# Four edits to the token-mixing stage of a two-layer decoder trunk: order of the chunk products, query sums in four column groups, a centred v, small projections in halves

## The chip, the cores and the metric

The kernel runs on one core of a Trainium2 chip. The metric is the device time in microseconds of one execution; lower is better. The core has TensorE (matmuls; "PE", with its weight loads as "PEld"), VectorE ("DVE"), ScalarE ("ACT"), GpSimd ("POOL") and SyncE ("SP"), which issues most of the transfers. Matmuls write to PSUM; VectorE and ScalarE move results from there to SBUF.

## The reference

Two layers, each a half-step SwiGLU block, a token-mixing block, and another half-step SwiGLU block, all on 512 tokens of width 1024 in float32. Only the mixing block is touched. It projects the normed tokens once and runs three kinds of heads side by side: sliding-window attention, RWKV-7 time mixing and a short gated convolution. What the change touches:

```python
q = rms_norm(q.reshape(B, T, ATT_Q_HEADS, HEAD_DIM), q_gain)      # 8 heads of 64
...
w_log = -softplus(-(w0 + tanh(wd) @ w_w2)) - 0.5                  # small projections of width 64
a = sigmoid(a0 + ad @ a_w2)
...
def step(S, inp):                                                 # state S: v x k, per head
    s_kk = einsum('bhvk,bhk->bhv', S, kk_t)
    S = (S * w_t[:, :, None, :] - s_kk[..., None] * (kk_t * a_t)[:, :, None, :]
         + v_t[..., None] * k_t[:, :, None, :])
    return S, einsum('bhvk,bhk->bhv', S, r_t)
...
mean = jnp.mean(y, axis=-1, keepdims=True)                        # over the 64 of a head
var = jnp.mean(jnp.square(y - mean), axis=-1, keepdims=True)
y = ((y - mean) * rsqrt(var + RWKV_GN_EPS)).reshape(...) * gn_w + gn_b
bonus = jnp.sum(r * k * r_k, axis=-1, keepdims=True) * v
y = (y + bonus) * g
```

Each row of the state S belongs to one element of v, and all rows go through the same linear step. So if the mean over a head's v is taken off every v_t before the recurrence, the mean of y over the head is zero at every step.

## The kernel before

Tokens lie along the free dimension (512 columns), channels along the 128 partitions. The mixing stage of a layer (`mix`) is a set of Python generators that a loop at its end advances in turn: `products` (the large input and output projections, the filler), `rwkv(0)` and `rwkv(1)` (two pairs of 64-wide time-mixing heads, one chain each) and `attention`. Each `yield` of a chain names a cost in microseconds; the loop lets `products` take as many steps as that cost buys, by `RWKV_WORK`, `ATT_WORK` and `FILL_WORK`. That sets the order in which instructions are traced; a scheduler in the build then fixes the order on every engine, letting earlier-traced instructions that it deems ready go first. Each engine runs its own list in order. A block under `tc.manual_schedule` keeps the order of TensorE's instructions within the block; `behind(m, other)` adds a dependence so that a group of matmuls becomes ready at once.

Products (`projector`, helper `mm6`, L98, and in other parts `mm3`, L90 to L92) split each operand into a high and a low part and take three matmuls of 128 x 128 weights and 256 moving columns for each half of the tokens. All small matmuls of the mixing stage are plain fp32; the trace shows two matmul instructions for each of them. Transposes show one.

What the change touches, in order of the work:

- In `products`, after the tiles of k and v come four query tiles, two heads each. A tile's square is summed over each head's 64 channels: four matmuls (one for each block of 128 tokens) with the squares as weights and the two-column constant `bones2` as the moving side (L615), then a square root on ScalarE (L616). `rq`, with tokens on partitions, is used in the softmax.
- `rwkv(q)` begins with two small projections, `ps_w` (L682) on partitions 0 to 63 and `ps_a` (L684) on 64 to 127.
- `pairs` (L733 to L747) multiplies, for each of 8 chunks of 64 tokens and each of the 2 heads, a 64 x 64 weight with 128 moving columns. `e` is the head and so the half of the array's rows; `c` is the chunk's parity and so the half of its columns. It runs twice a chain (`B`, `K`).
- `vN` (L799) is v with tokens on partitions: four transposes (`tmajor`, L784) and a ScalarE copy (`tcopy`, L789). `ps_xv` (L805) and the state products `ps_gn` and `ps_o` read it. The eliminations (L770, L771), 15 pairs of small VectorE instructions, invert 16 x 16 blocks in the meantime.
- `ps_s` (L889) and `ps_ys` (L895) carry the state over the chunks and give `y`. Then the head mean is summed with the constant `bones` (`headsum`, L539, tile `ps_m`) and taken off (L900); the variance follows in the same way (`ps_v`), then scale, shift, bonus and gate, ending at L916. The last output products need the `y` of both chains.

Of the kernel before, what the change touches and what calls it, by code (L numbers as in the profile page):

```python
# [11 lines left out]
AF = mybir.ActivationFunctionType  # L12
ALU = mybir.AluOpType
AXL = mybir.AxisListType
ORDER = mybir.DependencyInfo(mybir.DependencyClass.Sync, mybir.DependencyReason.DATA)

P = 128
D = 1024
T = 512
# [6 lines left out]
NB = T // P  # L26
CH = 64
NC = T // CH
HB = math.exp(-0.5) / 2
BASE = 16  # L30
PAD = 24
GAP = 448
GROUPS = ((0, 12), (12, 22))
RWKV_WORK, ATT_WORK, FILL_WORK = 29.8, 15.2, 129.6
# [2 lines left out]
def _columns(spec):  # L37
# [11 lines left out]
    ("cw", 6),  # L49
))  # L50
CON, NCON = _columns((
    ("ident", P), ("bones", P), ("bones2", 2), ("su", CH), ("iu", CH), ("diag", CH),
    ("lev0", CH), ("lev1", CH), ("i64", CH), ("mc", P), ("mp", P), ("mq", P),
))

# [2 lines left out]
def trunk_kernel(ctx, tc, ins, out, layers=L, phases=("ffn1", "mix", "ffn2")):  # L58
    nc = tc.nc
# [11 lines left out]
    tt, stt, ts = nc.vector.tensor_tensor, nc.vector.scalar_tensor_tensor, nc.vector.tensor_scalar  # L71
    act, mm = nc.scalar.activation, nc.tensor.matmul
# [7 lines left out]
    def psum(shape, name, tag="x"):  # L80
        return ps.tile(shape, F32, name=name, tag=tag, bufs=2)
# [27 lines left out]
    HALVES = (slice(0, T // 2), slice(T // 2, T))  # L109
    rows = (slice(0, CH), slice(CH, P))  # L110
# [4 lines left out]
    con = const.tile([P, NCON], F32, name="con")  # L115
# [18 lines left out]
    vals = {}  # L134
# [9 lines left out]
    def cst(name):  # L144
        a, b = CON[name]
        return con[:, a:b]
# [366 lines left out]
    def mix(l, hn, ss, mp, then):  # L513
# [17 lines left out]
        def EA(name):  # L531
            return mp.tile([P, T], F32, name=name, tag="ea", bufs=3)
# [4 lines left out]
        def headsum(src, name, tag="x"):  # L537
            pt = psum([P, T], name, tag)
            mm(pt, cst("bones"), src, start=True, stop=True)  # L539
            return pt  # L540
# [7 lines left out]
        blocks = lambda t: t.rearrange("p (b c) -> p b c", c=P)  # L548

        lw = mp.tile([P, 2 * P], F32, name="lw", tag="lw")  # L550
# [6 lines left out]
        k_, r_, v_, yr = {}, {}, {}, {}  # L557
# [8 lines left out]
        def products():  # L566
# [12 lines left out]
            pt = yield from tile_()  # L579
# [6 lines left out]
            sq = EA("ksq")  # L586
# [8 lines left out]
            pt = yield from tile_()  # L595
# [7 lines left out]
            nc.scalar.copy(V, pv)  # L603
            qr = mp.tile([P, 4, T], F32, name="qr", tag="qr")
            rq = small("rq", NB * 8)
            rq4 = rq.rearrange("p (b i g) -> p b i g", i=4, g=2)
            for i in range(4):
                pt = yield from tile_()
                nc.scalar.copy(qr[:, i], pt)
                sq = EA("qsq")  # L610
                act(sq, pt, AF.Square)
                yield
                pq = psum([P, NB, 2], "ps_q")
                for b in range(NB):
                    mm(pq[:, b], sq[:, b * P : (b + 1) * P], cst("bones2"), start=True, stop=True)  # L615
                act(rq4[:, :, i], pq, AF.Sqrt, bias=vals["eps64"])  # L616
            nc.vector.reciprocal(rq, rq)
            got.update(kt=kt, V=V, qr=qr, rq=rq)
            done.add("att")
# [14 lines left out]
            for q in range(2):  # L634
                pt = yield from tile_()
                cc = EA("conv_c")
                nc.scalar.copy(cc, pt)
                pt = yield from tile_()
                u = EA("conv_u")
# [5 lines left out]
                pt = yield from tile_()  # L645
# [12 lines left out]
            for i in range(KD - 2):  # L658
                w = load_w(wo1[l, i, :, :6], 6)
                pt = psmm()  # L660
# [13 lines left out]
        def rwkv(q):  # L674

            R = f"r{q}"
            c1 = slice(q, q + 1)
            cw = slice(q * P, (q + 1) * P)
            lo = got["lo"]

            pw = psum([P, T], "ps_w", R)
            mm(pw, lw[:64, cw], lo[:64], start=True, stop=True)  # L682
            pa = psum([P, T], "ps_a", R)
            mm(pa, lw[64:, cw], lo[64:], start=True, stop=True)  # L684
            yield 1.7
            kp = prm(l, "kk")[:, c1]
            sq = EQ(q, "kksq")
# [45 lines left out]
            def pairs(src, name, other):  # L733
                M = U(q, name, [P, 2, NB, 2, CH])
                pts = [psum([P, NB, 2, CH], "ps_c", R) for _ in range(2)]
                with tc.manual_schedule(engines={mybir.EngineType.PE}):
                    for b in range(NB):
                        for c in range(2):
                            n = 2 * b + c
                            for e in range(2):  # L740
                                m = mm(pts[e][rows[c], b], src[rows[e], n * CH : (n + 1) * CH], AR[rows[e], :, n], start=True, stop=True)
                                behind(m, other)
                msk = con[:, CON["su"][0] : CON["iu"][1]].unsqueeze(1).to_broadcast([P, NB, 2 * CH])
                for e in range(2):
                    other = tt(M[:, e].rearrange("p b a t -> p b (a t)"), pts[e].rearrange("p b a t -> p b (a t)"), msk, ALU.mult)
                yield 1.4
                return M, other  # L747
# [10 lines left out]
            for c in range(2):  # L758
                for m in range(NM):
                    n = (c * NM + m) * 2 * NB  # L760
# [6 lines left out]
            for s in range(BASE - 1):  # L767
                n = BASE - 1 - s
# [18 lines left out]
            def tcopy(src, name):  # L787
                t = blocks(S(q, name))
                nc.scalar.copy(t, tmajor(src, "ps_" + name))  # L789
                return t  # L790
# [5 lines left out]


            K_, other = yield from pairs(ka, "K", other)
            vN = tcopy(v_[q], "vN")  # L799
            yield 0.4  # L800
            px = psum([P, 2, NB, CH], "ps_xv", R)
            for e in range(2):
# [93 lines left out]
            tt(chunks(y)[:, 1:], chunks(y)[:, 1:], pt[:, 1:], ALU.add)  # L896
            yield 1.2

            pm = headsum(y, "ps_m", R)
            stt(y, pm, -1.0 / CH, y, ALU.mult, ALU.add)  # L900
            yield 0.9
            sq = EQ(q, "gnsq")
            act(sq, y, AF.Square)
            pv = headsum(sq, "ps_v", R)
# [310 lines left out]
def lay_out(i):  # L1215
    import numpy as np

    a = {}
    c = np.ascontiguousarray
    a["xT"] = c(i["x"][0].T).reshape(KD, P, T)  # L1220
    a["cT"] = c(i["c"].reshape(KD, P).T)


    wT = i["w_ada"].reshape(L, D, 9, KD, P).transpose(0, 2, 3, 4, 1)
    a["wadaT"] = c(wT)
    last = i["w_ada"][0, :, :D].reshape(KD, P, 4, 2, P)[:, :, :, 1].transpose(2, 1, 0, 3).reshape(4, P, D)
    a["wa0"] = c(np.stack([wT[0, 1, ::2], wT[0, 1, 1::2], wT[0, 0, ::2], last], axis=2))
    a["crep"] = c(np.broadcast_to(i["c"].reshape(1, D), (P, D)))
    for n, w in (("w1", "w_ffn1_in"), ("w2", "w_ffn2_in")):
        a[n + "i"] = c(i[w].reshape(L, KD, P, 2, NF, P)[:, :, :, :, :8].transpose(0, 4, 3, 2, 1, 5))  # L1230
        wp = i[w].reshape(L, 2, 4, P, 2, NF // 2, 2, P).transpose(0, 5, 4, 1, 3, 6, 2, 7)
        a[n + "p"] = c(wp.reshape(L, NF // 2, 2, 2, P, KD, P))
    for n, w in (("w1o", "w_ffn1_out"), ("w2o", "w_ffn2_out")):
        a[n] = c(i[w].reshape(L, NF, P, KD, P).transpose(0, 3, 2, 1, 4))

    pairs = np.concatenate([np.r_[g * CH : (g + 1) * CH] for t in range(4) for g in (t, 4 + t)])
    rw = lambda j: np.r_[768 + j * P : 768 + (j + 1) * P]
    cv = lambda j: np.r_[1792 + j * P : 1792 + (j + 1) * P]  # L1240
    order = [np.r_[512:768], pairs] + [rw(j) for j in (6, 2, 0, 4, 3, 1, 5, 7)]
    order += [cv(j) for j in (2, 4, 0, 3, 5, 1)]
    wm = i["w_mix_in"][:, :, np.concatenate(order)]
    a["wmi"] = c(wm.reshape(L, KD, P, 20, P).transpose(0, 3, 2, 1, 4))
    wo = i["w_mix_out"]
    w1 = wo[:, np.concatenate([pairs, np.r_[768:1024], np.r_[512:768]])]
    a["wmo1"] = c(w1.reshape(L, KD, P, KD, P).transpose(0, 3, 2, 1, 4))
    w2 = wo[:, 512:768, : 6 * P].reshape(L, 2, P, 2, 3, P)
    a["wmo2"] = c(w2.transpose(0, 3, 2, 4, 1, 5).reshape(L, 2, P, 6, P))
    a["lora"] = c(np.concatenate([i["rwkv_w_w2"], i["rwkv_a_w2"]], axis=1))  # L1250
    a["gw2"] = c(i["rwkv_g_w2"])

    def cols(v, n):
        return v.reshape(L, n, P).transpose(2, 0, 1)

    def twice(v):
        return np.concatenate([v, v], axis=1).T[:, :, None]

    sinks = i["att_sinks"][:, [0, 4, 1, 5, 2, 6, 3, 7]]
    a["par"] = c(np.concatenate([  # L1260
        cols(i["b_ada"], 72), cols(i["g_ffn1"], 8), cols(i["g_mix"], 8), cols(i["g_ffn2"], 8),
        twice(i["att_q_gain"]), twice(i["att_k_gain"]), np.broadcast_to(sinks[None], (P, L, 8)),
        cols(i["rwkv_mu"], 8), cols(i["rwkv_w0"], 2), cols(i["rwkv_a0"], 2), cols(i["rwkv_k_k"], 2),
        cols(i["rwkv_k_a"], 2), cols(i["rwkv_r_k"].reshape(L, 256), 2), cols(i["rwkv_gn_w"], 2),
        cols(i["rwkv_gn_b"], 2), cols(i["conv_w"].reshape(L, 768), 6),
    ], axis=2))


    r, s = np.arange(P)[:, None], np.arange(P)[None, :]
    u, v = r % CH, np.arange(CH)[None, :]  # L1270

    def lower(k, u, v):
        return (u >> (k + 1) == v >> (k + 1)) & ((u >> k) & 1 == 1) & ((v >> k) & 1 == 0)

    con = [r == s, r // CH == s // CH, r // CH == np.arange(2)[None, :], u < v, u <= v]
    con += [u // BASE == v // BASE, lower(4, u, v), lower(5, u, v)]
    con += [u == v, r <= s, r > s, s <= r]
    a["con"] = c(np.concatenate([np.asarray(x, np.float32) for x in con], axis=1))
    return a
# [16 lines left out]
```

## Time and profile before

| | |
|---|---|
| median of 3 runs | 1936.84 us (1936.34 to 1939.99) |
| profiled execution | 1942.73 us, span 1940.6 us |
| granted TensorE clock, mean | 0.990 |
| TensorE busy | 1894.4 us, 98% of the span |
| VectorE busy | 1400.0 us, 72% |
| ScalarE busy | 838.4 us, 43% |
| HBM traffic | 302.66 MB read, 3.41 MB written |

The time of an execution is a little longer than the span, which runs from the first to the last instruction. A busy TensorE includes matmuls that wait in its pipeline, so 98% does not say that the array works at its peak. The mixing stages lie at about 400 to 625 us and 1350 to 1576 us of the span. A line such as `ps_q<-con,qsq` names the tile written and the tiles read.

### The profile page before, as it was taken

How to read it: one execution, taken by the hardware profiler on the slowest of the kernel's cores; microseconds unless marked ns; L12 is line 12 of the kernel's file. 1: busy time of each engine (PE TensorE's matmuls, PEld its weight loads, DVE VectorE, ACT ScalarE, POOL GpSimd, SP SyncE). 2: the span in 40 equal slices, each digit the busy share in tenths (PEclk: the TensorE clock that was granted, in tenths of full speed). 3: DMA queues.
4: the chain of work that ended last, by engine and by line, in shares of the span. 5: the costliest groups of instructions: out<-in, count | busy, mean ns of one | idle time of the engine just before them, and what ended most of it. 6: DMA issues, size and time to landing. Idle time of an engine off the chain costs nothing. (4 is left out here: it accounts for less than half of the span.)

```text
span 1940.6 us, 36814 instructions
## 1 busy us (share of the span) xinstructions
PE 1894.4 (98%) x15392; PEld 1748.4 (90%) x15392; DVE 1400.0 (72%) x2176; ACT 838.4 (43%) x1269; POOL 130.8 (7%) x212
## 2 busy tenths in 40 slices
PE   8999999999999999999999999999999999999999
PEld 7998899797889999899899989988978899998997
DVE  7687687658975787677877776876588578773762
ACT  4443255347422554155345514544562235532551
POOL 0101101000000000110100020010000000010100
PEclk8999999999999999999999999999999999999999
DMA  7767875621222475886746688773222125765742
GB/s 296 250 161 232 258 197 170 211 69 47 54 60 63 133 203 168 279 216 173 227 123 180 171 263 234 184 221 97 88 54 57 51 61 153 205 218 131 197 113 90
DMA packets 104325, 308.44 MB, mean 159 GB/s; under 512 B 23392, under 2 KB 24416, under 8 KB 103136
## 3 DMA queue, kind: packets, MB, share of 16 engines
q1 hardware_dynamic: 75936, 203.34, 32.5%
q0 software_dynamic: 28224, 102.77, 21.5%
q8 instruction: 120, 1.97, 0.4%
q14 instruction: 45, 0.37, 0.1%
HBM read 302.66 MB, written 3.41 MB: 158 GB/s over the span
## 5 line engine op out<-in xcount | busy, mean ns | idle before, releaser
L101 ACT CAST wH<-wraw 128x1024 fp32r<-128x1024 f32 (+2 forms) x292 | 268.9, 922 | 561.7 <-PE ps_mm L91 157.5
L102 DVE TENSOR_TENSOR wL<-wraw,wH 128x1024 fp32r<-128x1024 f32 (+2 forms) x292 | 309.0, 1060 | 123.3 <-ACT wH L101 121.8
L91 PE MATMUL ps_mm<-actL,wH 128*128 128x512 f32 (+1 forms) x744 | 282.5, 380 | 0.0
L90 PE MATMUL ps_mm<-actH,wH 128*128 128x512 f32 (+1 forms) x744 | 282.5, 380 | 0.0
L92 PE MATMUL ps_mm<-actH,wL 128*128 128x512 f32 (+1 forms) x744 | 282.0, 379 | 0.0
L380 PE MATMUL ps_d<-comH,wH 128*128 128x256 f32 x816 | 227.6, 279 | 4.5 <-ACT s L402 3.8
L381 PE MATMUL ps_d<-comL,wH 128*128 128x256 f32 x816 | 226.2, 277 | 0.0
L382 PE MATMUL ps_d<-comH,wL 128*128 128x256 f32 x816 | 226.1, 277 | 0.0
L98 PE MATMUL ps_mm<-hnH,wH 128*128 128x256 f32 x1040 | 213.8, 287 | 5.3 <-ACT hnH L101 2.9
L98 PE MATMUL ps_mm<-hnH,wL 128*128 128x256 f32 x1040 | 213.9, 285 | 0.5 <-DVE wL L102 0.5
L98 PE MATMUL ps_mm<-hnL,wH 128*128 128x256 f32 x1040 | 212.5, 284 | 0.0
L163 DVE SCALAR_TENSOR_TENSOR wada<-wada,crep 128x1024 f32<-128x1024 f32 x140 | 167.8, 1221 | 53.8 <-DMA wada<-in_wadaT 53.6
L102 DVE TENSOR_TENSOR wL<-sum,wH 128x1024 fp32r<-128x1024 f32 x102 | 125.0, 1225 | 70.1 <-ACT wH L101 69.9
L98 PEld LDWEIGHTS ps_mm<-hnH,wH 128*128 128x128 f32 x1040 | 160.8, 191 | 13.6 <-issue 5.5
L101 ACT CAST wH<-sum 128x1024 fp32r<-128x1024 f32 x102 | 107.5, 1054 | 148.0 <-PE ps_d L381 72.1
L98 PEld LDWEIGHTS ps_mm<-hnH,wL 128*128 128x128 f32 x1040 | 161.2, 191 | 6.3 <-issue 4.7
L98 PEld LDWEIGHTS ps_mm<-hnL,wH 128*128 128x128 f32 x1040 | 161.6, 191 | 4.5 <-issue 3.9
L92 PEld LDWEIGHTS ps_mm<-actH,wL 128*128 128x128 f32 x744 | 141.2, 190 | 26.1
L91 PEld LDWEIGHTS ps_mm<-actL,wH 128*128 128x128 f32 x744 | 141.2, 190 | 25.6
L90 PEld LDWEIGHTS ps_mm<-actH,wH 128*128 128x128 f32 x744 | 140.9, 189 | 25.7
L380 PEld LDWEIGHTS ps_d<-comH,wH 128*128 128x128 f32 x816 | 153.9, 189 | 7.1 <-ACT s L402 5.0
L381 PEld LDWEIGHTS ps_d<-comL,wH 128*128 128x128 f32 x816 | 154.1, 189 | 0.0
(401 smaller groups left out, 4245.5 us busy)
## 6 DMA issues: line engine op xcount, KB each, us to landing
wada<-in_wadaT POOLq DMA_DIRECT2D x128, 512.0 KB, 5.0
wraw<-in_wmi SPq DMA_DIRECT2D x40, 512.0 KB
wraw<-in_w2p SPq DMA_DIRECT2D x36, 512.0 KB
wraw<-in_w1p SPq DMA_DIRECT2D x32, 512.0 KB
wraw<-in_w1o SPq DMA_DIRECT2D x32, 384.0 KB
wraw<-in_w2o SPq DMA_DIRECT2D x32, 384.0 KB
wraw<-in_w1i SPq DMA_DIRECT2D x20, 512.0 KB
wraw<-in_w1o SPq DMA_DIRECT2D x32, 320.0 KB
```

What stands on the lines that cost most here:

```text
L90: mm(acc, wH, xH, start=start, stop=False)
L91: mm(acc, wH, xL, start=False, stop=False)
L92: mm(acc, wL, xH, start=False, stop=stop)
L98: mm(acc[:, sl], w[a][:, k], x[b][:, sl], start=start and n == 0 and sl is HALVES[0], stop=stop and n == 2, skip_group_check=True)
L101: nc.scalar.copy(hi, src)
L102: nc.vector.tensor_sub(lo, src, hi.bitcast(F32))
L163: stt(w, w, 1.0, crep, ALU.mult, ALU.mult, accum_out=out_)
L380: mm(pt[:, i], wH, x[k][0], start=start and i + k == 0, stop=False, skip_group_check=True)
L381: mm(pt[:, i], wH, x[k][1], start=False, stop=False, skip_group_check=True)
L382: mm(pt[:, i], wL, x[k][0], start=False, stop=k == 3, skip_group_check=True)
```

## The change

Four edits, all in the mixing stage of both layers and both chains:

1. `pairs` loops over the head before the chunk's parity, so that neighbouring matmuls alternate between the column halves first.
2. The squares of all four query tiles are kept. One burst of four matmuls sums them, each with 32 columns of `bones` as weights (16 for each of the two heads) and 512 moving columns, each to its own 32 partitions. ScalarE copies the sums out, four transposes turn them, and one square root reads one of every 16 columns. `bones2` goes; `PAD` makes up for its two columns.
3. `vN` is centred when it is taken from PSUM: VectorE sums each head's 64 elements and subtracts the mean. The step that summed and subtracted the mean of `y` goes, with its `yield`. The bonus still reads the uncentred v.
4. The two small projections are cut in two halves of 256 tokens and issued alternately, in a fixed order.

```diff
@@ products
             rq = small("rq", NB * 8)
-            rq4 = rq.rearrange("p (b i g) -> p b i g", i=4, g=2)
+            sqs = []
             for i in range(4):
                 pt = yield from tile_()
                 nc.scalar.copy(qr[:, i], pt)
-                sq = EA("qsq")
-                act(sq, pt, AF.Square)
-                yield
-                pq = psum([P, NB, 2], "ps_q")
-                for b in range(NB):
-                    mm(pq[:, b], sq[:, b * P : (b + 1) * P], cst("bones2"), start=True, stop=True)
-                act(rq4[:, :, i], pq, AF.Sqrt, bias=vals["eps64"])
+                sqs.append(S(i % 2, "qsq"))
+                act(sqs[i], pt, AF.Square)
+            yield
+            pq = psum([P, T], "ps_q")
+            with tc.manual_schedule(engines={mybir.EngineType.PE}):
+                for i in range(4):
+                    mm(pq[32 * i : 32 * i + 32], cst("bones")[:, CH - 16 : CH + 16], sqs[i], start=True, stop=True)
+            qs = EA("qsum")
+            nc.scalar.copy(qs, pq)
+            yield
+            pq = psum([P, NB, P], "ps_qt")
+            for b in range(NB):
+                nc.tensor.transpose(pq[:, b], qs[:, b * P : (b + 1) * P], cst("ident"))
+            act(rq.rearrange("p (b i g) -> p b i g", i=4, g=2), pq.rearrange("p b (i g r) -> p b i g r", i=4, g=2)[:, :, :, :, 0], AF.Sqrt, bias=vals["eps64"])
             nc.vector.reciprocal(rq, rq)
@@ rwkv
-            pw = psum([P, T], "ps_w", R)
-            mm(pw, lw[:64, cw], lo[:64], start=True, stop=True)
-            pa = psum([P, T], "ps_a", R)
-            mm(pa, lw[64:, cw], lo[64:], start=True, stop=True)
+            pw, pa = (psum([P, T], n, R) for n in ("ps_w", "ps_a"))
+            with tc.manual_schedule(engines={mybir.EngineType.PE}):
+                for sl in HALVES:
+                    for pt, r in ((pw, rows[0]), (pa, rows[1])):
+                        mm(pt[:, sl], lw[r, cw], lo[r, sl], start=True, stop=True, skip_group_check=True)
@@ rwkv, pairs
                     for b in range(NB):
-                        for c in range(2):
-                            n = 2 * b + c
-                            for e in range(2):
+                        for e in range(2):
+                            for c in range(2):
+                                n = 2 * b + c
                                 m = mm(pts[e][rows[c], b], src[rows[e], n * CH : (n + 1) * CH], AR[rows[e], :, n], start=True, stop=True)
@@ rwkv
-            vN = tcopy(v_[q], "vN")
+            pt = tmajor(v_[q], "ps_vN").rearrange("p b (e d) -> p (b e) d", e=2)
+            mv = small(f"mv{q}", 2 * NB)
+            nc.vector.tensor_reduce(mv, pt, AXL.X, ALU.add)
+            vN = S(q, "vN")
+            stt(vN.rearrange("p (b d) -> p b d", d=CH), mv.unsqueeze(2).to_broadcast([P, 2 * NB, CH]), -1.0 / CH, pt, ALU.mult, ALU.add)
+            vN = blocks(vN)
@@ rwkv
-            pm = headsum(y, "ps_m", R)
-            stt(y, pm, -1.0 / CH, y, ALU.mult, ALU.add)
-            yield 0.9
             sq = EQ(q, "gnsq")
```

The constant table loses its `bones2` columns, and `PAD` goes from 24 to 26.

More of the change, by code (lines that the diff above doesn't have):

```diff
@@ L30 @@
 BASE = 16
-PAD = 24
+PAD = 26
 GAP = 448
@@ L51 @@
 CON, NCON = _columns((
-    ("ident", P), ("bones", P), ("bones2", 2), ("su", CH), ("iu", CH), ("diag", CH),
+    ("ident", P), ("bones", P), ("su", CH), ("iu", CH), ("diag", CH),
     ("lev0", CH), ("lev1", CH), ("i64", CH), ("mc", P), ("mp", P), ("mq", P),
@@ L1273, in lower @@
         return (u >> (k + 1) == v >> (k + 1)) & ((u >> k) & 1 == 1) & ((v >> k) & 1 == 0)
-    con = [r == s, r // CH == s // CH, r // CH == np.arange(2)[None, :], u < v, u <= v]
+    con = [r == s, r // CH == s // CH, u < v, u <= v]
     con += [u // BASE == v // BASE, lower(4, u, v), lower(5, u, v)]
```

## The prediction

> **What bounds the kernel now.** I read the page first, then the waits of TensorE, then stretches of the mixing stage, and last the timeline of TensorE around every burst that the change touches.
>
> ```profile
> PE 1894.4 (98%) x15392; PEld 1748.4 (90%) x15392; DVE 1400.0 (72%) x2176; ACT 838.4 (43%) x1269; POOL 130.8 (7%) x212
> ```
> ```profile
> PE ps_s L889 <- ACT y L884: 2.9, 2, 1.8
> ...
> PE ps_mm L98 <- DVE y L916: 0.5, 2, 0.3
> ```
> ```profile
> 480.00:520.00 40.00, 38.48 (x349) 31.11 (x348) 35.54 (x97) 21.71 (x54) 0.00 (x0) 1.00 0.21 52
> ```
> ```profile
> 1501.30:1511.50 10.20, 10.20 (x75) 8.29 (x75) 3.56 (x17) 1.27 (x3) 0.00 (x0) 0.50 0.04 9
> ```
> ```profile
> 550.20:560.00 9.80, 9.80 (x101) 8.10 (x98) 5.45 (x21) 3.45 (x8) 0.00 (x0) 1.00 0.07 12
> ```
>
> TensorE is busy 98% of the span, so a change is worth what it takes off TensorE's own sequence, minus any new gap. The waits (total, times, longest) show two small gaps that matter in mixing: ps_s waits for the eviction of y, 2.9 us in the two layers, and the last products wait 0.3 us a layer for the finished y of the second head pair. The third fence is a stretch of the first layer's mixing: the columns are length, then busy time of PE, weight loads, DVE, ACT, POOL, granted clock, DMA share, GB/s. DVE is busy 35.54 of 40 us there, close behind TensorE. The last two fences have the stretches right behind those gaps for ps_s: in the second layer, behind 1.8 us, the granted clock was 0.50 for 10.2 us, which costs 5.1 us of full-speed work; in the first, behind 1.1 us (2.9 less 1.8), it stayed at 1.00.
>
> The profiled execution took 1942.73 us, the median of the runs shown is 1936.84. Without that half-clock stretch it would be 1942.73 - 5.1 = 1937.6, next to the median, so I take it that the median run does not have the stretch, and set the sum against 1936.84. A measurement here can tell about 0.2%, 3.9 us, from no change.
>
> **How a burst is priced.** The products run as a stream of L98 matmuls, and small bursts break into it. The price of a burst is the time from a product row before it to one after it, less the products that started in that time. Two L98 matmuls take 0.23 us (612.19 to 612.42 below). So the price includes what it costs to enter and leave.
>
> **Query sums.** Before, each of four query tiles has a burst of its own: four fp32 sums, eight matmuls whose moving side is two columns wide. Columns: start, us, engine, line, what, count.
>
> ```profile
> 410.31 1.04 PE L615 MATMUL ps_q<-con,qsq 128*128 128x2 f32 x8
> 411.21 0.49 PE L98 MATMUL ps_mm<-hnH,wH 128*128 128x256 f32 x2
> ```
> ```profile
> 416.34 0.39 PE L98 MATMUL ps_mm<-hnL,wH 128*128 128x256 f32 x2
> 416.77 1.05 PE L615 MATMUL ps_q<-con,qsq 128*128 128x2 f32 x8
> 417.69 0.48 PE L98 MATMUL ps_mm<-hnH,wL 128*128 128x256 f32 x2
> 418.00 0.39 PE L98 MATMUL ps_mm<-hnH,wH 128*128 128x256 f32 x2
> ```
>
> The second burst costs 418.00 - 416.34 = 1.66, less four products (0.46), so 1.20 us. The first stands behind the transposes of v and shares their way in and out: 0.90 us from 410.31 to 411.21, of which I keep 0.80, since the transposes then have to leave by themselves. A layer has 0.80 + 3 x 1.20 = 4.40 us.
>
> After, one burst holds four matmuls of 128 rows x 32 columns with 512 moving columns, each in its own quarter of the columns, two passes each; then ScalarE copies the sums and four transposes turn them. No row has quarter-width column groups. The nearest is the attention's ps_av, two half-width groups with 512 moving columns; for the transposes it is ps_vN.
>
> ```profile
> 446.24 0.40 PE L98 MATMUL ps_mm<-hnL,wH 128*128 128x256 f32 x2
> 446.57 1.08 PE L990 MATMUL ps_av<-pmc,V 128*64 128x512 f32 x4
> 447.57 0.50 PE L98 MATMUL ps_mm<-hnH,wL 128*128 128x256 f32 x2
> 447.91 0.40 PE L98 MATMUL ps_mm<-hnH,wH 128*128 128x256 f32 x2
> ```
> ```profile
> 495.88 0.28 PE L98 MATMUL ps_mm<-hnH,wL 128*128 128x256 f32 x1
> 496.16 0.66 PE L784 MATMUL ps_vN<-con,v 128*128 128x128 f32 x4
> 496.57 0.37 PE L98 MATMUL ps_mm<-hnH,wL 128*128 128x256 f32 x1
> 496.77 0.40 PE L98 MATMUL ps_mm<-hnH,wH 128*128 128x256 f32 x2
> ```
> ```profile
> 612.19 0.39 PE L98 MATMUL ps_mm<-y2L,wH 128*128 128x256 f32 x2
> 612.42 0.40 PE L98 MATMUL ps_mm<-y2H,wL 128*128 128x256 f32 x2
> 612.65 1.02 PE L539 MATMUL ps_m<-y,con 128*128 128x512 f32 x2
> 613.11 0.80 PE L98 MATMUL ps_mm<-y3H,wH 128*128 128x256 f32 x2
> 613.75 0.39 PE L98 MATMUL ps_mm<-y3L,wH 128*128 128x256 f32 x2
> ```
>
> ps_av, four matmuls, costs 447.91 - 446.24 = 1.67 less 0.46, so 1.21 us. A single sum of the same width, ps_m, costs 613.75 - 612.42 = 1.33 less 0.46, so 0.87 us. Two of them apart would be 1.74; the two column groups ran together. I take 1.21 for the four quarters as well, because that row is the nearest; the other end is four in a row, 4 x 0.87 = 3.48. The transposes cost 496.77 - 495.88 = 0.89 less 0.23, so 0.66. New price of a layer 1.21 + 0.66 = 1.87, gain 4.40 - 1.87 = 2.53, **5.1 us for two layers**; at the other end 4.40 - 4.14 = 0.26 a layer, 0.5 us in all. The ScalarE copy between sums and transposes has the products as cover (one step is handed over there); two fewer steps are handed over in all, which only shifts the pacing. Scores need no rq, only the softmax does, so a later rq delays nothing at first.
>
> **No mean of y.** ps_m goes in two layers and two head pairs: 4 x 0.87 = **3.5 us off TensorE**. The DVE subtraction behind it goes too. In its place the eviction of ps_vN changes: one ScalarE copy becomes a DVE sum over the transposed v and a DVE subtraction.
>
> ```profile
> L900 DVE SCALAR_TENSOR_TENSOR y<-ps_m,y x4: 691/692/693, 557.6 to 1568.6; 128x512 f32<-128x512 f32 x4
> ...
> L953 DVE TENSOR_REDUCE mx<-Sc x16: 675/676/679, 435.2 to 1447.6; 128x4 f32<-128x512 f32 x16
> ...
> L789 ACT COPY vN<-ps_vN x4: 586/588/590, 496.9 to 1492.6; 128x512 f32<-128x512 f32 x4
> ```
>
> By these forms the step takes 0.676 + 0.692 instead of 0.588: 0.78 us longer before ps_xv can start, and 1.37 us more of DVE at that place, 0.69 less at the end. Behind it on DVE wait the softmax steps and the 16-row eliminations of the same head pair. Free it would be 0; exposed four times 4 x 0.78 = 3.1 us. The first pair's falls into the stretch where DVE is 89% busy, the second's behind it; so I charge 0.78 once a layer, **1.6 us**.
>
> **Small projections by halves.** Before, they ran apart for the first pair and together for the second:
>
> ```profile
> 461.18 1.12 PE L682 MATMUL ps_w<-lo,lw 64*128 64x512 f32 x2
> 462.23 0.66 PE L972 MATMUL ps_pt<-con,Sc 128*128 128x128 f32 x4
> 462.82 1.12 PE L684 MATMUL ps_a<-lo,lw 64*128 64x512 f32 x2
> ```
> ```profile
> 481.38 0.69 PE L682 MATMUL ps_w<-lo,lw 64*128 64x512 f32 x1
> 481.38 0.69 PE L684 MATMUL ps_a<-lo,lw 64*128 64x512 f32 x1
> ...
> 482.44 0.34 PE L741 MATMUL ps_c<-AR,a 64*64 64x128 f32 x4
> ```
>
> Transposes of the attention were put between ps_w and ps_a: 1.05 us each (461.18 to 462.23). The pair together takes 482.44 - 481.38 = 1.06. With the order held and the row halves alternating, the first pair saves 1.05 us a layer, **2.1 us**. If something is still put between after the first half, one quarter runs alone at each end: half of it, 1.05. The second pair gains nothing.
>
> **Chunk products, columns first.** The same matmuls in another order:
>
> ```profile
> 484.27 0.88 PE L741 MATMUL ps_c<-AR,a 64*64 64x128 f32 x22
> ```
> ```profile
> 542.31 0.30 PE L861 MATMUL ps_gn<-vN,kaN 64*64 64x64 f32 x8
> ```
>
> In the old order four of them last 0.34 us (the row at 482.44 above) and 22 are through in 0.88 us, so four run at a time: 18 more in 0.54 us is 0.12 us for every four. The ps_gn loop already has the new order (same rows, other columns next); with half the moving columns its eight are through in 0.30 us. Both orders fill the array; I take 0. If the new order ran two abreast, the eight fours of a call would take 0.12 us more each, 1.0 us a call and 7.7 us for the eight calls: the bad end. A tenth of that the other way, 0.8 us, is my good end, an estimate without a row.
>
> **The sum.** -5.1 - 3.5 - 2.1 + 0 + 1.6 = -9.1: 1936.84 - 9.1 = **1927.7 us**. Against the profiled execution's own time, half-clock stretch included, that is 1933.6.
>
> **Rivals.** *Column groups wait for each other.* Then the query sums give 0.5 instead of 5.1: 1927.7 + 4.6 = 1932.3 us. Against it stands ps_av. The Trainium skill, TensorE: Matmul & The Clock Gate, Part 3, states that a weight load overlaps a running matmul only where its row group differs, and quarters of the columns share all rows. By that rule this rival would be the forecast; ps_av and ps_gn, whose neighbours share rows and start together, speak against it for halves, and no row shows quarters.
>
> *A gap and the half clock (the other side).* ps_s waits because DVE works on the other pair's eliminations ahead of the eviction. If the added 1.37 us of DVE lengthens that gap in both layers and the clock falls each time as at 1501.30, this costs 2 x (1.4 + 5.1) = 13: 1927.7 + 13 = 1940.7, and with any further gap slower than 1936.84 + 3.9. It decides only if both layers do it in most runs; in one layer it gives 1934.2. For it: it happened once in the profile. Against: the shorter gap of the first layer left the clock at 1.00, and between the transposes of v (496.16) and that gap (ahead of 550.20) lies some 50 us of other work that can take up a delay. The Trainium skill, TensorE: Matmul & The Clock Gate, Part 1, has the clock fall only after an idle window of about 3.4 us; the trace has it fall behind a gap of 1.8 us, so I let the trace decide. By the page the rival would lose its 5.1 us a layer and end at 1930.5.
>
> *The chain becomes the end.* TensorE is freed of 10.7/2 = 5.3 us a layer, the second pair's chain only of 0.87 + 0.69 - 0.78 = 0.78, if its head does not move forward with the rest. Then products wait for y 4.5 us a layer: the row with 0.3 us grows, and -9.1 - 1.6 + 9.0 = -1.7 gives 1935.1 (the 1.6 charged above is in the 9.0). For it: that wait exists in both layers, so chain and products end together. Against: query sums and small projections lie ahead of the chain and move its head too.
>
> *Better.* The new order of work closes the ps_s gap: 2.9 us more, and 0.8 from the pairs, and part of the half-clock stretch where runs have it: about 1922.
>
> **Chances.** Forecast 0.49, columns wait 0.10, gap in one layer 0.13, in both 0.08, chain 0.12, better 0.08. Faster by over 0.2% (below 1933.0) are the forecast, the first rival, the better case and the upper part of the others, 0.69; within 0.2% are the chain and the single gap, 0.23; slower 0.08. The range 1922 to 1936 takes in the bounds and leaves out the double gap and half of the better case. The forecast's own range is 1924 to 1932.
>
> **What the profile after would show.** One ps_q burst a layer, four 32-column matmuls of two passes started within some 0.02 us of each other and a price near 1.2 us; started half a microsecond apart, the first rival. No ps_m, and y squared right after its last addition. ps_w and ps_a of the first pair together, about 1.06 us in all. The ps_c bursts as long as before. If ps_s or the product row behind L916 waits longer, or the half-clock share grows, the second or third rival holds. What would make the forecast wrong without any of them is a wholly new order of TensorE's work, in which other bursts are cut apart.

## The result and the profile after

Over 20 runs of each kernel the median went from 1936.81 us (1929.83 to 1942.88) to 1928.76 us (1920.99 to 1936.80): ratio 0.9964, 95% interval 0.9951 to 0.9976. In a later comparison it was 0.9942 (0.9922 to 0.9963). The forecast was 1927.7 us, so size and sign were right. Term by term it was not: the query sums gave less than forecast, the small projections about nothing on their own, the longer step of v showed no cost, and a gap that the sum had left in place closed.

The head of the page of the kernel after, profiled in an execution of 1928.72 us, and its waits (total, times, longest):

```profile
span 1926.7 us, 36742 instructions
PE 1886.0 (98%) x15360; PEld 1740.9 (90%) x15360; DVE 1401.6 (73%) x2180; ACT 835.2 (43%) x1261; POOL 130.7 (7%) x212
```
```profile
PE ps_bo L539 <- DVE bonus L725: 1.9, 4, 0.6
PE ps_x L841 <- DVE T L832: 1.8, 3, 1.0
PE ps_o L889 <- DVE N L879: 1.2, 2, 0.6
```

TensorE is still busy 98% of the span. The wait of ps_s for y, 2.9 us before, is gone from the list, and so is that of the last products for y (0.5 us). Small new ones came: ps_o for N 1.2, ps_x for T 1.8, and ps_bo rose from 1.3 to 1.9. The row of ps_bo before:

```profile
PE ps_bo L539 <- DVE bonus L717: 1.3, 4, 0.3
```

The two places of TensorE's timeline that the prediction had priced, in the first layer (start, us, engine, line, what, count):

```profile
421.98 0.39 PE L98 MATMUL ps_mm<-hnH,wL 128*128 128x256 f32 x2
422.30 1.06 PE L616 MATMUL ps_q<-qsq,con 128*32 128x512 f32 x6
423.29 0.50 PE L98 MATMUL ps_mm<-hnH,wH 128*128 128x256 f32 x2
...
424.56 1.05 PE L616 MATMUL ps_q<-qsq,con 128*32 128x512 f32 x2
...
426.34 0.60 PE L622 MATMUL ps_qt<-con,qsum 128*128 128x128 f32 x4
```
```profile
456.83 0.48 PE L692 MATMUL ps_w<-lo,lw 64*128 64x256 f32 x1
456.84 0.48 PE L692 MATMUL ps_a<-lo,lw 64*128 64x256 f32 x1
...
457.48 0.64 PE L982 MATMUL ps_pt<-con,Sc 128*128 128x128 f32 x4
458.05 0.48 PE L692 MATMUL ps_w<-lo,lw 64*128 64x256 f32 x1
458.06 0.48 PE L692 MATMUL ps_a<-lo,lw 64*128 64x256 f32 x1
...
477.49 0.59 PE L692 MATMUL ps_w<-lo,lw 64*128 64x256 f32 x2
...
497.82 0.70 PE L692 MATMUL ps_a<-lo,lw 64*128 64x256 f32 x2
```

Query sums: three quarters (six matmuls) ran as one burst, and products were put ahead of the fourth, which ran alone. Small projections: the first pair alternates, cut in the middle by the transposes of attention. In the second pair the last half of ps_a came 20 us after its partner, at 497.82.

### The profile page after: what moved, and what is told of

The parts are those of the page before. It is cut to its first block, busy times and chain, and to the rows that moved or that the text cites. A ratio compares the mean times of both kernels' runs of the same rounds, so it can differ in the third digit from the quotient of the medians.

```text
span 1926.7 us, 36742 instructions
## 1 busy us (share of the span) xinstructions
PE 1886.0 (98%) x15360; PEld 1740.9 (90%) x15360; DVE 1401.6 (73%) x2180; ACT 835.2 (43%) x1261; POOL 130.7 (7%) x212
## 5 line engine op out<-in xcount | busy, mean ns | idle before, releaser
L98 PE MATMUL ps_mm<-hnH,wH 128*128 128x256 f32 x1040 | 214.8, 287 | 5.1 <-ACT hnH L101 2.9
L98 PE MATMUL ps_mm<-hnL,wH 128*128 128x256 f32 x1040 | 212.5, 283 | 0.0
L98 PE MATMUL ps_mm<-hnH,wL 128*128 128x256 f32 x1040 | 210.0, 282 | 0.5 <-DVE wL L102 0.5
L98 PEld LDWEIGHTS ps_mm<-hnH,wH 128*128 128x128 f32 x1040 | 160.3, 190 | 16.0 <-issue 8.2
L98 PEld LDWEIGHTS ps_mm<-hnL,wH 128*128 128x128 f32 x1040 | 160.9, 190 | 6.7 <-issue 5.7
L98 PEld LDWEIGHTS ps_mm<-hnH,wL 128*128 128x128 f32 x1040 | 160.4, 191 | 4.0 <-issue 2.9
```

Source lines behind the costliest of these rows:

```text
L98: mm(acc[:, sl], w[a][:, k], x[b][:, sl], start=start and n == 0 and sl is HALVES[0], stop=stop and n == 2, skip_group_check=True)
```

## How the runs are compared

Each run has a span and a mean granted TensorE clock. The runs of one kernel spread over 8 to 18 us where there are twelve or more, and part of that comes with the clock. I call span times clock the time at full clock: an estimate that treats the span as all TensorE, which it is to 98%. The column of that name is its difference to the kernel before in the same comparison, with its standard error (the first row borrows the 35 runs of before from the second).

The last column looks at the two mixing stages alone, in the one profile of each kernel: the time from the first L98 row of a stage to the last L98 row that reads yr, with stretches at clock 0.50 counted at half, summed over the layers, as a difference to 443.6 us before. Before, these rows start at 407.38 and 629.73, and at 1358.06 and 1584.47 with 10.24 us at half clock between them; after, at 404.90 and 623.09, and at 1349.97 and 1567.09. Two profiles of one kernel differ by 0.1 us (QC and QC_fill), 0.4 (together_Q and together_2) and 1.3 (after and after_2). What lies outside these stages differs by up to 7.6 us between the profiles, although no edit is made there, so the last column is the sharper one for what an edit does inside them.

In the names, "Q" is the query sums, "C" the centred v, "O" the chunk order, "H" the halves; the edits are the parts of the diff above.

| kernel | median us (runs) | ratio to before, 95% | clock | at full clock | mixing stages, one profile |
|---|---|---|---|---|---|
| after | 1928.76 (20) | 0.9964 (0.9951 to 0.9976) | 0.9911 | -6.6 ± 0.7 | -8.3 |
| only_Q | 1937.35 (12) | 1.0003 (0.9987 to 1.0019) | 0.9902 | -0.2 ± 0.8 | -3.2 |
| only_C | 1935.90 (12) | 0.9989 (0.9971 to 1.0008) | 0.9899 | -2.9 ± 0.8 | -3.6 |
| only_O | 1938.38 (12) | 1.0005 (0.9991 to 1.0018) | 0.9904 | -0.1 ± 0.7 | -0.3 |
| only_H | 1934.25 (12) | 0.9988 (0.9974 to 1.0003) | 0.9914 | -0.6 ± 0.6 | -0.7 |
| QC | 1938.36 (12) | 0.9991 (0.9977 to 1.0004) | 0.9874 | -5.9 ± 0.8 | -7.8 |
| without_C | 1943.46 (12) | 1.0022 (1.0000 to 1.0044) | 0.9886 | +0.7 ± 0.9 | -0.3 |
| together_Q | 1928.16 (6) | 0.9942 (0.9923 to 0.9961) | 0.9908 | -9.2 ± 1.0 | -8.5 |
| best3 | 1938.34 (12) | 0.9995 (0.9978 to 1.0012) | 0.9878 | -5.7 ± 0.9 | -6.8 |
| QC_idle | 1939.52 (12) | 1.0013 (0.9993 to 1.0033) | 0.9902 | +2.0 ± 0.9 | -0.1 |
| together_2 | 1928.95 (6) | 0.9948 (0.9929 to 0.9967) | 0.9903 | -9.4 ± 0.8 | -8.1 |
| after_2 | 1928.35 (7) | 0.9942 (0.9922 to 0.9963) | 0.9917 | -8.0 ± 1.3 | -9.7 |

The kernel before stood at a clock of 0.9904, 0.9901 and 0.9904 in the three comparisons.

## The experiments

**One part alone.** Four kernels, each the kernel before with one part of the diff.

```diff
 only_Q: sqs, ps_q in four column groups, qsum, ps_qt
 only_C: mv and the subtraction in front of vN; no ps_m behind y
 only_O: for e in range(2): for c in range(2)   (ps_c)
 only_H: for sl in HALVES: ps_w, ps_a
```

> Only the query sums in column groups. Prices theory (what leaves TensorE's sequence is what the time loses): three quarters together and one apart as in the changed kernel, 1.21 + 1.21, and 0.66 for the transposes, against 4.40 before: 1.3 us a layer, 2.6 us in all, ratio 0.9987; the waits for ps_s stay near 2.9 us. Gap theory (the time came from the vanished wait for ps_s and the half clock behind it): no gain as long as that wait stands, ratio 1.000; 3 us or more if it goes.

> Only the centred v and no mean of y. Prices theory: 4 x 0.87 = 3.5 us less on TensorE, up to 1.6 us given back if the longer step for v shows, so 1.9 to 3.5 us, ratio 0.9982 to 0.9990. Gap theory: if this is the edit that moves VectorE's eliminations off the wait for ps_s, that wait falls from 2.9 us to under 0.5 and the time by 3.5 + 2.9 = 6.4 us or more, ratio 0.9967 or lower.

> Only the order of the chunk products. Prices theory: fours run together in either order, so ps_c takes as long as before, under 0.5 us in all, ratio 1.000. Order theory (neighbours that share columns are slower): ps_c takes 0.2 to 0.8 us less, ratio 0.9996. Gap theory: 1.000 with the wait for ps_s in place.

> Only the small projections in halves. Prices theory: the first pair takes 0.65 + 0.62 instead of 2.10 us, 0.8 less a layer; in the second pair the last quarter is put far behind the others and costs 0.86 us by itself, so about nothing is left, ratio 1.000. Prediction on record: 2.1 us, ratio 0.9989. Gap theory: 1.000 unless the wait for ps_s goes.

At full clock the four give -0.2, -2.9, -0.1 and -0.6, together -3.8, beside -6.6 and -8.0 for the whole change; the noise of such a sum is about 2 us. By the mixing stages they give -3.2, -3.6, -0.3 and -0.7, together -7.8, beside -8.3 and -9.7. So it is not shown that the four parts fail to add up. Their waits show what each part moves. TensorE's waits in only_Q, then in only_C, then in only_H:

```profile
PE ps_bo L539 <- DVE bonus L724: 2.4, 4, 0.9
...
PE ps_mm L98 <- DVE y L923: 1.8, 2, 0.9
PE ps_s L896 <- ACT y L891: 1.0, 1, 1.0
```
```profile
PE ps_s L894 <- ACT y L889: 3.6, 2, 1.8
...
PE ps_o L881 <- DVE N L871: 2.7, 2, 1.4
```
```profile
PE ps_w L848 <- DVE TT L841: 0.9, 2, 0.4
PE ps_mm L98 <- DVE y L917: 0.6, 2, 0.3
```

In only_Q the products wait 1.8 us for y (0.5 before) and ps_bo 2.4 (1.3 before): TensorE gets to the tail sooner than the chain, as the third rival has it. But ps_s waits only 1.0 us (2.9 before), so the three rows together grow by 0.5 us, which does not explain why the runs show -0.2 where the price of two bursts is -2.6 and the stages show -3.2; that difference stays open. In only_C that wait for y is gone, but ps_o and ps_s wait 2.7 and 3.6 us, 3.4 more than before: the longer step of v is exposed there. In only_H the wait of ps_s is gone, although nothing near it was edited; ps_w waits 0.9 us for TT instead, and at full clock next to nothing is won. The chunk order alone is worth nothing.

**Two parts, and all but one.** QC has the query sums and the centred v, and the old projections and order; without_C has everything but the centred v.

```diff
 QC:        before + (ps_q, ps_qt) + (mv, vN, no ps_m)
 without_C: after - (mv, vN); ps_m and its subtraction as before
```

> Query sums and centred v together, without the other two edits. Chain theory (the query sums alone are taken back because the chain of the second head pair, which they do not shorten, then ends last; with the centred v that chain is shorter and the gain comes through): more than the two alone, 2.6 + 3.5 = 6.1 us, ratio 0.9969, and no wait of products for y. Additive theory (each edit gives what it gave alone): 0.9992, and the rest of the whole change's gain needs the other two edits.

> The changed kernel without its third edit: y keeps its mean step, v is not centred. Chain theory: TensorE is freed by the query sums and by the first pair's halves, but products wait for y, over 1 us in the two layers together, and the time stays within 2 us of before, ratio 0.999 to 1.001. Additive theory: 0.9 us less than before by the sum of what the other three gave alone, 0.9996, with no longer wait for y. Prices theory without a chain: 2.6 us less, 0.9987.

QC is 5.9 us better than before at full clock, close to the 6.1 of the chain theory, and its time is within the noise of before, because its clock fell from 0.9901 to 0.9874: 1936 us times 0.0027 is 5.2 us. That fall was in neither theory. Without C nothing is left at full clock (+0.7), and the ratio is 1.0022 (1.0000 to 1.0044). The waits of QC, then of without_C:

```profile
PE ps_s L901 <- ACT y L896: 3.4, 2, 1.7
...
PE ps_o L888 <- DVE N L878: 2.7, 2, 1.4
```
```profile
PE ps_mm L98 <- DVE y L924: 1.8, 2, 0.9
PE ps_s L897 <- ACT y L892: 1.6, 2, 1.3
```

QC has no row of products waiting for y; without_C has the same 1.8 us as only_Q. Does Q pay only where C has shortened the chain? By the runs Q gives 0.2 us alone and 3.0 on top of C (5.9 less 2.9); that difference, 2.8 us, has a standard error of 1.4. The mixing stages give 3.2 alone and 4.2 on top of C, so it is not shown. That the whole change needs C is beyond doubt: +0.7 against -6.6 and -8.0 by the runs, -0.3 against -8.3 and -9.7 by the stages.

**The query sums kept together.** A dependence makes all four matmuls follow the last square, so that no work can be put between them. best3 has it too, and does the second pair's projections at full width, as before.

```diff
 together_Q:
-                act(sqs[i], pt, AF.Square)
+                sqd = act(sqs[i], pt, AF.Square)
...
-                    mm(pq[32 * i : 32 * i + 32], ..., sqs[i], start=True, stop=True)
+                    behind(mm(pq[32 * i : 32 * i + 32], ..., sqs[i], start=True, stop=True), sqd)
 best3, in addition:
-                for sl in HALVES:
+                for sl in (ALL,) if q else HALVES:
```

> The changed kernel with one dependence more: all four query sums become ready together and stand side by side. If the four quarters run at once: one burst a layer at 1.2 us instead of two, starts within 0.03 us, 2.4 us less than the changed kernel, ratio to before 0.9952 (0.9964 - 0.0012). If the fourth has to wait for the others: a burst of 2.1 us or more, and the ratio of the changed kernel, 0.9964.

> As the one before, and the second head pair's small projections in full width again (halves for the first pair alone). If the lone last quarter of the second pair is what the halves give back: 0.86 us a layer less, 1.7 in all, ratio 0.9943. If that quarter was hidden: 0.9952.

TensorE's timeline of together_Q at the query sums:

```profile
422.53 0.39 PE L98 MATMUL ps_mm<-hnL,wH 128*128 128x256 f32 x2
422.96 1.06 PE L616 MATMUL ps_q<-qsq,con 128*32 128x512 f32 x8
423.96 0.50 PE L98 MATMUL ps_mm<-hnH,wL 128*128 128x256 f32 x2
424.30 0.40 PE L98 MATMUL ps_mm<-hnH,wH 128*128 128x256 f32 x2
...
438.58 0.51 PE L98 MATMUL ps_mm<-hnH,wH 128*128 128x256 f32 x2 [1.35 <-DVE lo L563]
```

Eight matmuls in one burst, 424.30 - 422.53 - 0.46 = 1.31 us: the price of a pair of half-width groups (1.21), not of four sums in a row (3.48). The first passes of the four start within 0.02 us of each other. The first rival is refuted. But the forecast gain of 2.4 us on after shows neither in the later times (together_2 and after_2 below: 0.9948 and 0.9942) nor in the stages (-8.5 and -8.1 beside -8.3 and -9.7). A new wait of some 1.35 us follows in each layer, in the first at 438.58, where the finished lo is late. At full clock together_Q is ahead by 2.6 and then 1.4 us, with standard errors of 1.2 and 1.5, so a part of the gain is not excluded.

best3 differs from together_Q in one place, and its time is about 10 us worse, which neither of its theories had. Of this, the clock (0.9878 beside 0.9908) makes 5.8 us and the time at full clock 3.5. Its waits, then VectorE's timeline of it and, below that, of after:

```profile
PE ps_s L902 <- ACT y L897: 3.2, 2, 1.7
...
PE ps_o L889 <- DVE N L879: 2.7, 2, 1.4
```
```profile
540.83 0.16 DVE L778 TENSOR_TENSOR elim<-G,inv 64x15 f32<-64x15 f32 x1
...
542.71 0.41 DVE L878 TENSOR_TENSOR GT<-ps_gn,con 128x256 f32<-128x256 f32 x1
...
547.71 0.74 DVE L896 TENSOR_TENSOR RT<-ps_o,AR 128x256 f32<-128x256 f32 x2
```
```profile
537.81 0.16 DVE L778 TENSOR_TENSOR elim<-G,inv 64x15 f32<-64x15 f32 x1
...
543.38 0.41 DVE L878 TENSOR_TENSOR GT<-ps_gn,con 128x256 f32<-128x256 f32 x1
...
546.50 0.76 DVE L896 TENSOR_TENSOR RT<-ps_o,AR 128x256 f32<-128x256 f32 x2 [0.45 <-PE ps_o L894]
```

In best3 the second pair's eliminations begin at 540.83, 1.9 us ahead of GT (the first pair's eviction of ps_gn), and RT, which y and so ps_s wait for, stands behind them: the last step ahead of it starts at 547.58. In after they begin at 537.81, 5.6 us ahead of GT; 24 of the steps run without a break before GT, and VectorE is idle 0.45 us ahead of RT. together_Q has the same lead (536.75 and 542.32) and the same 0.45 us. So the halves of the second pair pull that pair's chain forward and take the waits of ps_s and part of ps_o away. That is where their gain is, most of it through the clock, and not in the length of their own bursts.

**The half clock.** QC_idle is QC with work meant for its gaps: matmuls of 512 columns, read by nobody, seven behind ps_gn and eight behind ps_o of the first pair. together_2 is together_Q and after_2 is after, unchanged, for the same comparison; QC_fill is QC, unchanged.

```diff
 QC_idle:
+        def idle(n):
+            pt = psum([P, T], "ps_idle") if n else None
+            for _ in range(n):
+                mm(pt.rearrange(...), ones_r, ones_r.unsqueeze(1).to_broadcast([P, 4, P]), start=True, stop=True)
...
+                idle(7 if q == 0 else 0)      # behind ps_gn
+                idle(8 if q == 0 else 0)      # behind ps_o
```

> A second profile of query sums and centred v together, for its two gaps and its clock: waits for ps_s and ps_o of some 6 us in the two layers, and a half-clock stretch behind at least one of them.

> Query sums and centred v, plus work that nobody reads: behind ps_gn and ps_o of the first pair stand 7 and 8 more matmuls of 512 columns, 1.5 and 1.7 us, that fill TensorE's two gaps of a layer. Clock theory (the gaps cost twice: TensorE waits, and the clock then falls to half): the time at full clock stays as it was, the mean clock rises from 0.987 to about 0.991, and the time falls by some 5 us although more is computed, ratio 0.996 to 0.997. Prices theory alone (more work, more time; the clock falls where it likes): no gain, 0.999 to 1.001.

> All four edits and the query sums held together, once more, beside the changed kernel on the same chip: by the prices 2.4 us less than that one; by its first timing 0.9942 of the kernel before.

> The changed kernel once more, for the comparison: 0.9964 of the kernel before, clock 0.991, time at full clock 6 to 7 us less than before.

QC_fill ran once, 1938.42 us at a clock of 0.986, with half-clock stretches behind the gaps of both layers again; ps_s and ps_o wait 6.0 us in all. Stretches (length, busy PE, weight loads, DVE, ACT, POOL, clock, DMA share, GB/s) of QC in both layers, then of QC_idle at the first of these places:

```profile
545.29:548.70 3.41, 1.80 (x16) 1.37 (x16) 2.73 (x14) 1.29 (x3) 0.00 (x0) 0.99 0.00 0
548.70:552.10 3.40, 3.40 (x21) 2.62 (x20) 0.58 (x3) 0.59 (x1) 0.00 (x0) 0.50 0.12 26
...
1497.59:1501.00 3.41, 2.25 (x22) 1.75 (x23) 2.43 (x13) 1.29 (x3) 0.00 (x0) 1.00 0.00 0
1501.00:1504.40 3.40, 3.40 (x19) 2.72 (x19) 0.79 (x3) 0.59 (x1) 0.00 (x0) 0.50 0.12 24
```
```profile
545.20:548.60 3.40, 2.27 (x25) 1.52 (x23) 3.02 (x15) 0.70 (x2) 0.00 (x0) 1.00 0.00 0
548.60:552.00 3.40, 3.30 (x41) 2.67 (x42) 0.99 (x4) 1.23 (x3) 0.00 (x0) 1.00 0.10 22
```

The stretch is gone in both layers, and the clock is back at 0.9902. But the idle matmuls did not fill the gaps. In QC, ps_xv and other ready work stand behind ps_gn; in QC_idle idle matmuls stand there, and most of that work comes later. The waits of ps_o and ps_s went from 6.1 us only to 4.4, with the longest down from 1.7 to 0.9, and nearly all of the idle work was added to the sequence:

```profile
PE ps_o L894 <- DVE N L884: 1.9, 2, 0.9
...
PE ps_s L908 <- ACT y L903: 1.3, 2, 0.7
PE ps_s L908 <- DVE St L909: 1.2, 2, 0.6
```
```profile
L550 PE MATMUL ps_idle<-ones_r 128*128 128x512 f32 x30 | 8.0, 407 | 0.0
```

They are busy for 8.0 us in the two layers, and the time at full clock rose by 7.9 us against QC (+2.0 and -5.9; by the stages 7.7), where the clock theory had it unchanged. The experiment shows the half clock going with the longest gaps. It does not show that busy time decides: TensorE is busy 2.27 us of the window in QC_idle, and was 2.25 in QC's second layer, where the clock fell. As a remedy it gives back what it wins.

No version clearly beats after. together_Q, twice compared, ties with it: 0.9942 and 0.9948 beside 0.9964 and 0.9942.

## Why the prediction was right, point by point

**Query sums, -5.1: the term was mis-sized; two bursts come to -2.6.** The price of a burst was right (1.21 forecast; 1.31 with four quarters). The count of bursts was wrong: the step took it that the four sums stand together, since their order is held. It holds against each other only; the order of the build put products in front of the fourth, whose square came later. Two bursts at about 1.2 and the transposes at 0.66 are 3.1 us a layer against 4.40, so 1.3 a layer. The mixing stages show 3.2 us in all for Q alone. Kept together, the sums and transposes come to 1.31 and 0.66, so 2.4 a layer, nearly as forecast, but then meet the wait for lo.

**No mean of y, -3.5: right as far as it can be told.** only_C gives -2.9 ± 0.8 at full clock and -3.6 by its stages, with the longer step of v in it.

**The longer step of v, +1.6: not separable, and no cost shows.** With it, the third edit was to give -1.9; only_C gives more, as above. The new operations last what the prediction took from the rows of other operations (0.676 and 0.692). VectorE's timeline of after:

```profile
535.67 0.68 DVE L809 TENSOR_REDUCE mv<-ps_vN 128x8 f32<-128x512 f32 x1
536.39 0.69 DVE L811 SCALAR_TENSOR_TENSOR vN<-mv,ps_vN 128x512 f32<-128x512 f32 x1
```

What it costs depends on the neighbours: in only_C the waits of ps_o and ps_s rise by 3.4 us, in after they fall by 1.7. The waits of only_C and its -2.9 do not close by rows: -3.5, -0.5 for the wait for y and +3.4 would be -0.6. Over 2 us stay without a row.

**Small projections, -2.1: wrong as a price, about 0.** The first pair was cut after the first half, as the prediction allowed, so it gives 0.8 us a layer: bursts from 456.83 to 457.48 and, by the same length, at 458.05, 2 x 0.65 against 2 x 1.05. The step that failed is "the second pair gains nothing": it loses, since half of ps_a runs alone 20 us later. Its row, 0.70 us long, and the products around it give a price of some 0.8, and only_H as a whole -0.6 ± 0.6. The gain of this edit is in what it moves, and that step was not in the prediction's sum.

**Chunk order, 0: right** (only_O -0.1 ± 0.7).

**Rivals.** *Column groups wait for each other*: refuted by the burst of together_Q. The Trainium skill, TensorE: Matmul & The Clock Gate, Part 3, has weight loads overlap only where row groups differ; here quarters that share all rows cost 1.31 us together, where one sum alone costs 0.87. *The chain becomes the end*: seen where C is missing, at 0.9 us a layer instead of the 4.5 forecast, and not in the whole. *A gap and the half clock*: true of QC and of best3, whose clocks are 0.9874 and 0.9878. It did not decide here because the halves of the second pair, which the prediction thought idle, removed the gap. *Better* had 0.08: its mechanism, the closed gap of ps_s, is what happened. The 2.9 us of that wait do not show as such, for only_H closed it too and gave -0.6 ± 0.6; what shows is some clock (0.9904 to 0.9911, 1.4 us; 2.5 in the later comparison).

So the sum was right partly by luck. By the stages of the single parts, the query sums gave 1.9 us less than forecast and the projections 1.4 less; the third edit gave 1.7 more, and the clock, which the sum left out, 1.4 or more. Errors of both signs met.

The prediction set its sum against the median because it took the median run to lack the half-clock stretch of the profiled one. The clocks do not bear that out: 0.990 in the profiled execution, 0.9904 in the mean of 35 others. Against the profiled execution's own time, the same sum gave 1933.6; the profiled execution after took 1928.72. What else made the profiled execution of before longer stays open.

## What to carry to other kernels

Price an edit by its bursts, but then ask which other stream it moves: here an edit worth about nothing by its own bursts made 10 us of difference, more than half of it through the clock, by shifting when a second chain reaches VectorE. Test parts in combination: without C the other three gained nothing, and with them C was worth over 7 us instead of some 3. Time the changed stage beside the execution: the same part showed 0.2 us over twelve runs and 3.2 in its own stages. In QC, with gaps of 1.4 and 1.7 us in each layer, the granted clock took 5.2 us; such gaps are better closed with useful work moved forward, for idle matmuls cost what they saved.

## What was not expected of the hardware

The half-clock stretches begin on a fixed grid within an execution. Those of QC begin at 548.7, 692.0, 982.2, 1043.6, 1330.3, 1501.0 and 1644.3 us; counted from the one at 378.0, these are 50.0, 92.0, 177.0, 195.0, 279.0, 329.0 and 371.0 steps of 3.413 us. The kernel before and after stand on such a grid too, each with its own beginning. So whether a gap lowers the clock may depend on how it falls into the grid, which is argued and not shown. best3 has nearly the same gaps in both layers; the windows ahead of and behind them:

```profile
545.40:548.80 3.40, 1.86 (x52) 1.52 (x42) 3.04 (x14) 0.65 (x2) 0.00 (x0) 1.00 0.02 5
548.80:552.20 3.40, 3.40 (x34) 2.60 (x30) 1.64 (x8) 1.23 (x3) 0.00 (x0) 1.00 0.09 24
...
1494.29:1497.70 3.41, 1.71 (x38) 1.34 (x28) 2.92 (x14) 0.70 (x2) 0.00 (x0) 1.00 0.02 5
1497.70:1501.10 3.40, 3.40 (x19) 2.63 (x20) 1.36 (x7) 0.59 (x1) 0.00 (x0) 0.50 0.05 13
```

TensorE was busy 1.86 us of the window in the first layer, and the clock stayed; 1.71 us in the second, and it fell for 10.2 us. In QC it fell behind 2.25 us as well, and in QC_idle it stayed behind 2.27, so these figures give no rule by busy time alone; what counts in a window stays open. The Trainium skill, TensorE: Matmul & The Clock Gate, Part 1, tells of a free-running window of 3413 ns, which the grid bears out, and of a fall after an idle window of about 3.4 us, which it does not: none of the windows shown was idle, and the widest gap in them was 1.7 us. With a new phase in each execution, this would also explain why runs of one kernel differ by some us along with their clock; that was only argued.
